# Maps of a differential attention summed without reciprocals, head outputs scaled on ScalarE, and a one-operation rope rotation

## The chip, the core and the metric

One core of a Trainium2 chip runs the whole kernel. The metric is the device time of one execution in microseconds (us), lower is better. Engines are named as the profile names them: PE is TensorE, DVE is VectorE, ACT is ScalarE, POOL is GpSimd, SP is SyncE, which issues most DMAs.

## The reference

The kernel computes one decoder layer on 512 tokens of 1024 features: a recurrent branch and a differential attention branch from one input projection, merged by gates, then a squared-ReLU MLP. The attention is what the change touches. Each of 8 heads has two softmax maps over the same values, and the second map is subtracted with a learned factor before the head's RMS norm:

```python
q = apply_rope(rms_norm(q.reshape(B, S, N_HEADS, 2, HEAD_DIM)) * q_norm_gain[l], cos, sin)
...
lam = (jnp.exp(jnp.sum(lambda_q1[l] * lambda_k1[l])) - jnp.exp(jnp.sum(lambda_q2[l] * lambda_k2[l])) + lam_init)
...
s = jnp.einsum("bhcqd,bhckd->bhcqk", qi, kt).astype(jnp.float32) * scale
p = jax.nn.softmax(jnp.where(mask, s, -jnp.inf), axis=-1)
attn = p[:, :, 0] - lam * p[:, :, 1]
o = jnp.einsum("bhqk,bhkv->bhqv", attn, vt)
...
o = rms_norm(o) * subln_gain * (1.0 - lam_init)

def apply_rope(x, cos, sin):
    x1, x2 = x[..., : HEAD_DIM // 2], x[..., HEAD_DIM // 2:]
    return jnp.concatenate([x1 * cos - x2 * sin, x2 * cos + x1 * sin], axis=-1)
```

## The kernel before

All large products run on PE as three fp32r matmuls each (`mm3`, L127 to L131): every operand is split into a high and a low part. For weights `load_w` (L114 to L125) does this: a DMA brings 128x1024 floats, ACT casts them to `wh` (L122) and DVE subtracts to get `wl` (L123), both at high priority. Nearly every 24 matmuls of 128x512 need one such pair, so ACT and DVE serve PE all through the program.

Until about 170 us the kernel projects the inputs of the recurrent branch and the first quarter of q and k. `qk_quarter` (L509 to L537) makes a quarter token-major in four tiles `raw` of 128x512, and turns each by the rope: L528 is issued twice for a tile, once for each half of 32 of every 64 columns (the halves swapped times the sine table, into `qsq`), L530 multiplies by the cosine, L531 adds, and a reciprocal square root of 32 columns (`rsqrt`, L84 to L100) scales the tile in L535. Quarter 0 is done before 124 us, quarters 1, 2 and 3 later. `qk_transpose` (L539 to L567) turns the tiles by PE (L547).

From about 170 to 447 us the 8 heads run (`heads`, L720 to L751), interleaved with other PE work that `fill` (L696 to L718) hands out by the table `PLAN`: gates `gm`, scans of the recurrent branch (L461, L462, L471), the other quarters, the values, the projection of the recurrent branch. `UNITS` sets how much of it is emitted between two steps of a head. Then the order on each engine is a list scheduler's, which takes instructions by priority and by estimated readiness, so that one edit can move many neighbours.

Each head has four steps `i`, for 128 queries each, with n = 128, 256, 384 or 512 keys. `softmax_step` (L572 to L598): PE makes the two maps of scores (`sc`), DVE adds the mask and finds the row's extreme (L587, into `e` and `nm`), ACT takes the exponential and its row sum (L589), DVE forms the reciprocals of both sums (L593) and the coefficient `cc` = s0 · nlam / s1 (L595), and L596 sums the maps as e0 + cc·e1. The result is s0 times the wanted map. `weights_t` transposes it by PE (L604, `aT`) and copies it out on ACT (odd steps, L607) or DVE (even steps, L609); `value_step` multiplies with the values (`po`, L615). A step's transposes and values come one step later in the program, so that PE has other work meanwhile.

`head_norm` (L618 to L636) ends a head: ACT copies the 128x512 output (`o`, L622) and takes four row sums of squares of 128x128 (`osq`, L625); DVE multiplies them by the squared reciprocals (L629, L630), takes the reciprocal square root (ten small operations, L89 to L99), multiplies by the reciprocal again (L633) and scales the output in one operation of 128x512 (L635). `head_out` (L638 to L647) transposes it by PE (L642, `yT`) in the next head's third step; for head 7 only after the gates that are left.

Of the kernel before, what the change touches and what calls it, by code (L numbers as in the profile page):

```python
# [20 lines left out]
AF = mybir.ActivationFunctionType  # L21
ALU = mybir.AluOpType
AX = mybir.AxisListType

P = 128
# [3 lines left out]
TB = S // P  # L29
# [24 lines left out]
def build(tc, out, x, xT_in, c, pos, vecs, reps, ada, w_xr, w_xr7, w_qk, w_v, w_gr, w_gm, w_lru,  # L54
# [4 lines left out]
    with ExitStack() as es:  # L59
# [18 lines left out]
        def tiny(name, n, dt=F32):  # L78
            return tmp.tile([P, n], dt, name=name, tag=f"s{n}", bufs=4 if n >= 32 else 12)
# [5 lines left out]
        def rsqrt(dst, src, n, mul, eps, name):  # L85

            eng = nc.vector
            v = tiny(name + "v", n)
            eng.tensor_scalar(v, src, mul, eps, op0=ALU.mult, op1=ALU.add)  # L89
            y = tiny(name + "y0", n, I32)  # L90
# [418 lines left out]
        def qk_quarter(qt):  # L509
# [10 lines left out]
            for t in range(TB):  # L520
                raw = rot[t]
                sqt = t_(f"qsq{qt}_{t}", tag="r")
                nc.scalar.activation(sqt, raw, AF.Square)
                nc.vector.tensor_reduce(s2[:, t * 8:t * 8 + 8], g8(sqt), axis=AX.X, op=ALU.add)
                r4, s4 = v4(raw), v4(sqt)
                for hf in range(2):
                    a, b = slice(hf * 32, hf * 32 + 32), slice(32 - hf * 32, 64 - hf * 32)
                    nc.vector.tensor_tensor(s4[:, :, :, a], r4[:, :, :, b],  # L528
                                            st[:, t, :, None, a].to_broadcast([P, 2, 4, 32]), op=ALU.mult)
                nc.vector.tensor_tensor(r4, r4, ct[:, t, :, None, :].to_broadcast([P, 2, 4, 64]), op=ALU.mult)  # L530
                nc.vector.tensor_tensor(raw, raw, sqt, op=ALU.add)  # L531
# [39 lines left out]

        def softmax_step(hd, q, k, i, rr):  # L572

            n = (i + 1) * P
            nn = max(n, 256)
            qc = slice(i * P, (i + 1) * P)
            sums = tiny(f"sm{hd}_{i}", 2)
            es_ = []
# [5 lines left out]
            for m in range(2):  # L584
# [4 lines left out]
                nc.scalar.activation(e[:, :n], e[:, :n], AF.Exp, bias=nm, scale=-1.0,  # L589
                                     accum_out=sums[:, m:m + 1])  # L590
                es_.append(e)
            rc = rr[:, 2 * i:2 * i + 2]
            nc.vector.reciprocal(rc, sums)  # L593
            cc = tiny(f"cc{hd}_{i}", 1)
            nc.vector.scalar_tensor_tensor(cc, sums[:, 0:1], nlam, rc[:, 1:2], op0=ALU.mult, op1=ALU.mult)  # L595
            nc.vector.scalar_tensor_tensor(es_[0][:, :n], es_[1][:, :n], cc, es_[0][:, :n],  # L596
# [20 lines left out]

        def head_norm(hd, po, rr):  # L618

# [4 lines left out]
            for t in range(TB):  # L624
                nc.scalar.activation(osq[:, t * P:(t + 1) * P], o1[:, t * P:(t + 1) * P], AF.Square,  # L625
                                     accum_out=os_[:, t:t + 1])
            r0 = rr[:, 0:8:2]
            o2 = tiny(f"o2{hd}", 4)
            nc.vector.tensor_tensor(o2, r0, r0, op=ALU.mult)  # L629
            nc.vector.tensor_tensor(o2, o2, os_, op=ALU.mult)  # L630
            orr = tiny(f"or{hd}", 4)
            rsqrt(orr, o2, 4, 1.0 / P, EPS, f"or{hd}")
            nc.vector.tensor_tensor(orr, orr, r0, op=ALU.mult)  # L633
            o3 = lambda t: t.rearrange("p (a b) -> p a b", b=P)
            nc.vector.tensor_tensor(o3(o1), o3(o1), orr[:, :, None].to_broadcast([P, TB, P]), op=ALU.mult)  # L635
            return o1  # L636
# [83 lines left out]
        def heads():  # L720
# [5 lines left out]
            for hd in range(NH):  # L726
                while hd // 2 not in qks or hd // 4 not in vs:
                    yield "need"
                q, k = qks[hd // 2][hd % 2]
                rr = tiny(f"rr{hd}", 8)  # L730
                po = None
                for i in range(TB):
                    a = softmax_step(hd, q, k, i, rr)
                    yield hd
# [13 lines left out]
                todo = []  # L748
                out_ = head_norm(hd, po, rr)
                yield hd  # L750
# [387 lines left out]
```

## Time and profile before

| | |
|---|---|
| median of 3 runs | 877.9 us (876.23 to 878.12) |
| the profiled execution | 876.41 us |
| its span | 874.6 us, so 1.81 us lie around it |
| granted TensorE clock | 1.00 in every slice |
| busy PE, DVE, ACT | 861.0, 651.5, 449.2 us |
| chain that ended last | PE 86%, DVE 10%, ACT 1%, DMA 1% |

PE is busy for 98% of the span; nearly 7 us of its idle time lie in the first 12 us and 3 us in the last 15. A matmul of 128x512 is shown as longer than the distance to the next, since the rows of two overlap; so an idle entry ahead of one shows only what of a wait is over that overlap. DVE and ACT are idle for a quarter and a half of the span on average, but not evenly: there are stretches in which both are full. The chain names DVE where the last thing before a matmul was a DVE result.

### The profile page before, as it was taken

How to read it: one execution, taken by the hardware profiler on the slowest of the kernel's cores; microseconds unless marked ns; L12 is line 12 of the kernel's file. 1: busy time of each engine (PE TensorE's matmuls, PEld its weight loads, DVE VectorE, ACT ScalarE, POOL GpSimd, SP SyncE). 2: the span in 40 equal slices, each digit the busy share in tenths (PEclk: the TensorE clock that was granted, in tenths of full speed). 3: DMA queues.
4: the chain of work that ended last, by engine and by line, in shares of the span. 5: the costliest groups of instructions: out<-in, count | busy, mean ns of one | idle time of the engine just before them, and what ended most of it. 6: DMA issues, size and time to landing. Idle time of an engine off the chain costs nothing.

```text
span 874.6 us, 11292 instructions
## 1 busy us (share of the span) xinstructions
PE 861.0 (98%) x4012; PEld 705.5 (81%) x4012; DVE 651.5 (74%) x1251; ACT 449.2 (51%) x748; POOL 15.1 (2%) x50
## 2 busy tenths in 40 slices
PE   6999999999999999999999999999999999999998
PEld 3888887877878888888888888888888888888887
DVE  6997995599859855786758556858766885876397
ACT  6673547985536543535623343747545544554461
POOL 1000000000000000000000000000000000002110
PEclk9999999999999999999999999999999999999999
DMA  8979425412255372238336332822641344139572
GB/s 315 370 250 319 152 97 134 136 68 73 87 131 169 99 191 76 93 87 227 110 126 210 132 121 75 273 87 72 193 148 70 128 161 169 49 126 235 120 122 96
DMA packets 64572, 128.92 MB, mean 147 GB/s; under 512 B 6146, under 2 KB 30850, under 8 KB 64516
## 3 DMA queue, kind: packets, MB, share of 16 engines
q1 hardware_dynamic: 59236, 122.97, 43.3%
q0 software_dynamic: 5280, 5.24, 3.9%
q8 instruction: 31, 0.51, 0.2%
q14 instruction: 25, 0.20, 0.1%
HBM read 113.51 MB, written 2.10 MB: 132 GB/s over the span
## 4 chain that ended last, share of the span: by engine, by line
PE 86%; DVE 10%; DMA 1%; issue 1%; ACT 1%; SPq 1%; ACTq 0%; DVEq 0%
PE f L131 6%; PE f L129 6%; PE f L130 6%; PE X L131 3%; PE X L130 3%; PE X L129 3%; PE gm L129 3%; PE gm L130 3%; PE gm L131 3%; DVE wl L123 2%; PE sc L582 2%; PE qk L131 2%; PE qk L129 2%; PE qk L130 2%; PE xr L129 2%; PE pr L129 2%
## 5 line engine op out<-in xcount | busy, mean ns | idle before, releaser
L122 ACT CAST wh<-w 128x1024 fp32r<-128x1024 f32 (+1 forms) x113 | 118.0, 1044 | 214.5 <-issue 48.1
L123 DVE TENSOR_TENSOR wl<-w,wh 128x1024 fp32r<-128x1024 f32 (+1 forms) x113 | 137.0, 1213 | 68.1 <-ACT wh L122 64.5
L131 PE MATMUL f<-h2h,wl 128*128 128x512 f32 x240 | 93.5, 390 | 0.4 <-DVE wl L123 0.4
L130 PE MATMUL f<-h2l,wh 128*128 128x512 f32 x240 | 93.2, 389 | 0.0
L129 PE MATMUL f<-h2h,wh 128*128 128x512 f32 x240 | 92.9, 390 | 0.0
L131 PEld LDWEIGHTS f<-h2h,wl 128*128 128x128 f32 x240 | 45.0, 188 | 10.1 <-DVE wl L123 0.8
L130 PEld LDWEIGHTS f<-h2l,wh 128*128 128x128 f32 x240 | 45.1, 188 | 9.4
L129 PEld LDWEIGHTS f<-h2h,wh 128*128 128x128 f32 x240 | 45.0, 188 | 9.3
L130 PE MATMUL gm<-hl,wh 128*128 128x512 f32 x128 | 51.0, 398 | 0.0
L129 PE MATMUL qk<-wh,hh 128*128 128x512 f32 x128 | 50.7, 396 | 0.0
L129 PE MATMUL gm<-hh,wh 128*128 128x512 f32 x128 | 50.5, 394 | 0.0
L131 PE MATMUL gm<-hh,wl 128*128 128x512 f32 x128 | 50.5, 394 | 0.0
L131 PE MATMUL qk<-wh,hl 128*128 128x512 f32 x128 | 50.4, 394 | 0.0
L130 PE MATMUL qk<-wl,hh 128*128 128x512 f32 x128 | 50.4, 394 | 0.0
L941 DVE TENSOR_TENSOR p_1l<-b,p_1h 128x1024 fp32r<-128x1024 f32 x24 | 29.4, 1223 | 26.3 <-ACT p_1h L940 26.1
L589 ACT ACTIVATE e<-e,nm 128x128 f32<-128x128 f32 (+3 forms) x64 | 35.7, 559 | 24.4 <-DVE nm L587 24.4
L940 ACT CAST p_1h<-b 128x1024 fp32r<-128x1024 f32 x24 | 25.2, 1051 | 31.0 <-PE f L130 22.9
L941 DVE TENSOR_TENSOR p_0l<-b,p_0h 128x1024 fp32r<-128x1024 f32 x24 | 29.3, 1223 | 15.0 <-ACT p_0h L940 13.8
L587 DVE CUSTOM_DVE_ANT_0 e<-sc,mask 128x128 f32<-128x128 f32 (+3 forms) x64 | 30.3, 484 | 9.9 <-PE sc L582 9.9
L940 ACT CAST p_0h<-b 128x1024 fp32r<-128x1024 f32 x24 | 25.3, 1055 | 24.2 <-PE X L131 12.4
L188 DVE CUSTOM_DVE_ANT_0 ada<-ada,cb,bada 128x1024 f32<-128x1024 f32 x16 | 20.5, 1283 | 14.3 <-DMA ada<-in_ada 14.1
L984 DVE TENSOR_TENSOR b<-b,b 128x1024 f32<-128x1024 f32 x24 | 29.1, 1220 | 0.1
(444 smaller groups left out, 2216.9 us busy)
## 6 DMA issues: line engine op xcount, KB each, us to landing
ada<-in_ada SPq DMA_DIRECT2D x64, 256.0 KB, 5.8
w<-in_w_ff SPq DMA_DIRECT2D x32, 512.0 KB, 3.2
b<-in_w_ff SPq DMA_DIRECT2D x30, 512.0 KB, 3.4
w<-in_w_qk SPq DMA_DIRECT2D x16, 512.0 KB, 3.2
w<-in_w_gm SPq DMA_DIRECT2D x16, 512.0 KB, 3.7
ada<-in_ada SPq DMA_DIRECT2D x16, 512.0 KB, 3.3
b_t<-in_w_ff POOLq DMA_DIRECT2D x10, 512.0 KB, 6.5
w<-in_w_gr SPq DMA_DIRECT2D x8, 512.0 KB, 4.0
```

Source lines behind the costliest of these rows:

```text
L122: i_w = nc.scalar.copy(wh[:, :n], w[:, :n])
L123: nc.vector.tensor_tensor(wl[:, :n], w[:, :n], f32(wh)[:, :n], op=ALU.subtract)
L129: nc.tensor.matmul(ps, lh, rh, start=first, stop=False, skip_group_check=more)
L130: nc.tensor.matmul(ps, lh, rl, start=False, stop=False, skip_group_check=more)
L131: nc.tensor.matmul(ps, ll, rh, start=False, stop=last, skip_group_check=more)
L188: nc.vector.tensor_tensor_reduce(w, w, cb, 1.0, bada[:, col:col + 1], op0=ALU.mult, op1=ALU.add, accum_out=mod[:, col:col + 1])
L582: nc.tensor.matmul(ps[m][:, :nn], q[m][:, qc], k[m][r][:, :nn], start=r == 0, stop=r == 1)
L587: nc.vector.tensor_tensor_reduce(e[:, :n], ps[m][:, :n], mask[:, S - n:], 1.0, 1e30, op0=ALU.add, op1=ALU.min, accum_out=nm)
L589: nc.scalar.activation(e[:, :n], e[:, :n], AF.Exp, bias=nm, scale=-1.0, accum_out=sums[:, m:m + 1])
L940: nc.scalar.copy(v4(wh), v)
L941: nc.vector.tensor_tensor(v4(wl), v, f32(v4(wh)), op=ALU.subtract)
L984: nc.vector.tensor_tensor(d, d, s_, op=ALU.add)
```

## The change

In `rsqrt` the first scaling is left out if no factor is given. In the rope one 128x512 operation, which reads the swapped halves through a reversed axis, takes the place of the two of 128x256. In `softmax_step` the maps are summed without reciprocals, as s1·e0 + (nlam·s0)·e1: ACT scales `e0` by s1 in place and forms `cc` = nlam·s0, so L593 and L595 are gone. The result is now s0·s1 times the wanted map, and `head_norm` sets it right: the small number of the norm is multiplied by (s0·s1)², in three operations on 128x4, and the output is scaled by ACT, four times 128x128. Lines of the change are shifted by up to two against those before.

```diff
--- before.py
+++ after.py
@@ -85,8 +85,10 @@
         def rsqrt(dst, src, n, mul, eps, name):
 
             eng = nc.vector
-            v = tiny(name + "v", n)
-            eng.tensor_scalar(v, src, mul, eps, op0=ALU.mult, op1=ALU.add)
+            v = src
+            if mul is not None:
+                v = tiny(name + "v", n)
+                eng.tensor_scalar(v, src, mul, eps, op0=ALU.mult, op1=ALU.add)
             y = tiny(name + "y0", n, I32)
             eng.tensor_scalar(y, v.bitcast(I32), -0.5, float(RSQRT_MAGIC), op0=ALU.mult, op1=ALU.add)
             y = y.bitcast(F32)
@@ -523,10 +525,9 @@
                 nc.scalar.activation(sqt, raw, AF.Square)
                 nc.vector.tensor_reduce(s2[:, t * 8:t * 8 + 8], g8(sqt), axis=AX.X, op=ALU.add)
                 r4, s4 = v4(raw), v4(sqt)
-                for hf in range(2):
-                    a, b = slice(hf * 32, hf * 32 + 32), slice(32 - hf * 32, 64 - hf * 32)
-                    nc.vector.tensor_tensor(s4[:, :, :, a], r4[:, :, :, b],
-                                            st[:, t, :, None, a].to_broadcast([P, 2, 4, 32]), op=ALU.mult)
+                sw = lambda t: t.rearrange("p m g (h d) -> p m g h d", h=2)
+                nc.vector.tensor_tensor(sw(s4), sw(r4)[:, :, :, ::-1, :],
+                                        sw(st[:, t, :, None, :].to_broadcast([P, 2, 4, 64])), op=ALU.mult)
                 nc.vector.tensor_tensor(r4, r4, ct[:, t, :, None, :].to_broadcast([P, 2, 4, 64]), op=ALU.mult)
                 nc.vector.tensor_tensor(raw, raw, sqt, op=ALU.add)
             rq = tiny(f"rq{qt}", 32)
@@ -569,12 +570,11 @@
         def att(name, dt=F32):
             return t_(name, dt, "a")
 
-        def softmax_step(hd, q, k, i, rr):
+        def softmax_step(hd, q, k, i, sums):
 
             n = (i + 1) * P
             nn = max(n, 256)
             qc = slice(i * P, (i + 1) * P)
-            sums = tiny(f"sm{hd}_{i}", 2)
             es_ = []
             ps = [bank(f"sc{hd}_{i}_{m}", "sc", 2) for m in range(2)]
             for m in range(2):
@@ -587,12 +587,11 @@
                 nc.vector.tensor_tensor_reduce(e[:, :n], ps[m][:, :n], mask[:, S - n:], 1.0, 1e30,
                                                op0=ALU.add, op1=ALU.min, accum_out=nm)
                 nc.scalar.activation(e[:, :n], e[:, :n], AF.Exp, bias=nm, scale=-1.0,
-                                     accum_out=sums[:, m:m + 1])
+                                     accum_out=sums[:, 2 * i + m:2 * i + m + 1])
                 es_.append(e)
-            rc = rr[:, 2 * i:2 * i + 2]
-            nc.vector.reciprocal(rc, sums)
+            nc.scalar.activation(es_[0][:, :n], es_[0][:, :n], AF.Copy, scale=sums[:, 2 * i + 1:2 * i + 2])
             cc = tiny(f"cc{hd}_{i}", 1)
-            nc.vector.scalar_tensor_tensor(cc, sums[:, 0:1], nlam, rc[:, 1:2], op0=ALU.mult, op1=ALU.mult)
+            nc.scalar.activation(cc, sums[:, 2 * i:2 * i + 1], AF.Copy, scale=nlam)
             nc.vector.scalar_tensor_tensor(es_[0][:, :n], es_[1][:, :n], cc, es_[0][:, :n],
                                            op0=ALU.mult, op1=ALU.add)
             return es_[0]
@@ -615,7 +614,7 @@
                 nc.tensor.matmul(po[:, i * P:n], aT[:, j * P:(j + 1) * P], v[j][:, vc * P:(vc + 1) * P],
                                  start=(j == 0), stop=(j == i))
 
-        def head_norm(hd, po, rr):
+        def head_norm(hd, po, sums):
 
             o1 = t_(f"o1{hd}")
             os_ = tiny(f"os{hd}", 4)
@@ -624,15 +623,16 @@
             for t in range(TB):
                 nc.scalar.activation(osq[:, t * P:(t + 1) * P], o1[:, t * P:(t + 1) * P], AF.Square,
                                      accum_out=os_[:, t:t + 1])
-            r0 = rr[:, 0:8:2]
-            o2 = tiny(f"o2{hd}", 4)
-            nc.vector.tensor_tensor(o2, r0, r0, op=ALU.mult)
-            nc.vector.tensor_tensor(o2, o2, os_, op=ALU.mult)
+            pp = tiny(f"op{hd}", 4)
+            nc.vector.tensor_tensor(pp, sums[:, 0:8:2], sums[:, 1:8:2], op=ALU.mult)
+            nc.vector.scalar_tensor_tensor(pp, pp, EPS, pp, op0=ALU.mult, op1=ALU.mult)
+            v = tiny(f"orv{hd}", 4)
+            nc.vector.scalar_tensor_tensor(v, os_, 1.0 / P, pp, op0=ALU.mult, op1=ALU.add)
             orr = tiny(f"or{hd}", 4)
-            rsqrt(orr, o2, 4, 1.0 / P, EPS, f"or{hd}")
-            nc.vector.tensor_tensor(orr, orr, r0, op=ALU.mult)
-            o3 = lambda t: t.rearrange("p (a b) -> p a b", b=P)
-            nc.vector.tensor_tensor(o3(o1), o3(o1), orr[:, :, None].to_broadcast([P, TB, P]), op=ALU.mult)
+            rsqrt(orr, v, 4, None, None, f"or{hd}")
+            for t in range(TB):
+                ob = o1[:, t * P:(t + 1) * P]
+                nc.scalar.activation(ob, ob, AF.Copy, scale=orr[:, t:t + 1])
             return o1
 
         def head_out(hd, o1):
@@ -727,10 +727,10 @@
                 while hd // 2 not in qks or hd // 4 not in vs:
                     yield "need"
                 q, k = qks[hd // 2][hd % 2]
-                rr = tiny(f"rr{hd}", 8)
+                sums = tiny(f"sm{hd}", 8)
                 po = None
                 for i in range(TB):
-                    a = softmax_step(hd, q, k, i, rr)
+                    a = softmax_step(hd, q, k, i, sums)
                     yield hd
                     if i == 0:
                         po = bank(f"po{hd}", "o", 1)
@@ -746,7 +746,7 @@
                     d()
                     yield hd
                 todo = []
-                out_ = head_norm(hd, po, rr)
+                out_ = head_norm(hd, po, sums)
                 yield hd
             y_att[NH - 1] = head_out(NH - 1, out_)
```

The order of the instructions moves too. First ACT at head 0, steps 0 and 1 (names: e, head, step, map; L589 the exponentials, L685 a gate, L460 and L462 a part of a scan, wh a weight's cast). Before:

```order
L589 ACTIVATE e0_0_0_1758,sm0_0_1750<-e0_0_0_1758,nm0_0_0_1757 128x128
L589 ACTIVATE e0_0_1_1762,sm0_0_1750<-e0_0_1_1762,nm0_0_1_1761 128x128
L685 ACTIVATE m0_0_1769<-gm0_1776 128x512
L460 ACTIVATE r0_1395<-r0_1395,sp8_705 128x512
L122 CAST wh28_1966<-w28_1964 128x1024
L589 ACTIVATE e0_1_0_1811,sm0_1_1803<-e0_1_0_1811,nm0_1_0_1810 128x256
L589 ACTIVATE e0_1_1_1815,sm0_1_1803<-e0_1_1_1815,nm0_1_1_1814 128x256
L460 ACTIVATE r1_1442<-r1_1442,sp8_705 128x512
L685 ACTIVATE m0_1_1869<-gm1_1876 128x512
```

With the change:

```order
L589 ACTIVATE e0_0_0_1753,sm0_1745<-e0_0_0_1753,nm0_0_0_1752 128x128
L589 ACTIVATE e0_0_1_1757,sm0_1745<-e0_0_1_1757,nm0_0_1_1756 128x128
L594 ACTIVATE cc0_0_1761<-sm0_1745,nlam_633 128x1
L592 ACTIVATE e0_0_0_1753<-e0_0_0_1753,sm0_1745 128x128
L685 ACTIVATE m0_0_1764<-gm0_1771 128x512
L124 CAST wh28_1958<-w28_1956 128x1024
L589 ACTIVATE e0_1_0_1805,sm0_1745<-e0_1_0_1805,nm0_1_0_1804 128x256
L589 ACTIVATE e0_1_1_1809,sm0_1745<-e0_1_1_1809,nm0_1_1_1808 128x256
L594 ACTIVATE cc0_1_1813<-sm0_1745,nlam_633 128x1
L592 ACTIVATE e0_1_0_1805<-e0_1_0_1805,sm0_1745 128x256
L462 ACTIVATE r0_1391<-r0_1391,sp8_705 128x512
```

Each step's coefficient and scaling come on ACT behind its second exponential, ahead of the gate and the cast.

Second, DVE at head 0, step 2: from the second map's mask to the sum of the maps (L596 before, L595 now; xc are the scans). Before:

```order
L587 ISA e0_2_1_1855,nm0_2_1_1854<-sc0_2_1_1845,mask_104 128x384
L587 ISA nm0_2_1_1854 128x1
L471 TENSOR_TENSOR xc1_1088<-xc1_1088,gel1_1086 128x512
L461 SCALAR_TENSOR_TENSOR xc2_1126<-r2_1563,xc2_1126 128x512
L123 TENSOR_TENSOR wl29_2109<-w29_2106,wh29_2108 128x1024
L143 TENSOR_TENSOR yl1_1841<-xc1_1088,yh1_1839 128x512
L593 RECIPROCAL rr0_1749<-sm0_2_1843 128x2
L462 SCALAR_TENSOR_TENSOR xc2_1126<-r2_1563,xc2_1126 128x512
L595 SCALAR_TENSOR_TENSOR cc0_2_1859<-sm0_2_1843,nlam_633,rr0_1749 128x1
L587 ISA e0_3_0_1943,nm0_3_0_1942<-sc0_3_0_1936,mask_104 128x512
L587 ISA nm0_3_0_1942 128x1
L596 SCALAR_TENSOR_TENSOR e0_2_0_1851<-e0_2_1_1855,cc0_2_1859,e0_2_0_1851 128x384
```

With the change:

```order
L587 ISA e0_2_1_1848,nm0_2_1_1847<-sc0_2_1_1838,mask_104 128x384
L587 ISA nm0_2_1_1847 128x1
L463 SCALAR_TENSOR_TENSOR xc0_1046<-r0_1391,xc0_1046 128x512
L463 SCALAR_TENSOR_TENSOR xc1_1084<-r1_1438,xc1_1084 128x512
L464 SCALAR_TENSOR_TENSOR xc0_1046<-r0_1391,xc0_1046 128x512
L464 SCALAR_TENSOR_TENSOR xc1_1084<-r1_1438,xc1_1084 128x512
L473 TENSOR_TENSOR xc0_1046<-xc0_1046,gel0_1044 128x512
L473 TENSOR_TENSOR xc1_1084<-xc1_1084,gel1_1082 128x512
L595 SCALAR_TENSOR_TENSOR e0_2_0_1844<-e0_2_1_1848,cc0_2_1852,e0_2_0_1844 128x384
```

Six operations of two scans now stand together between the mask and the sum, where before there were a part of two scans, a weight's subtraction, and the other map's masks.

Third, DVE at the end of quarter 1's rope: from the last sum of a rope (raw, L531 before) to the first scaled tile (L535 before), which PE transposes at 246.6 us. Before:

```order
L531 TENSOR_TENSOR raw1_3_2343<-raw1_3_2343,qsq1_3_2366 128x512
L95 TENSOR_TENSOR rq1a0_2378<-rq1y0_2376 128x32
L98 SCALAR_TENSOR_TENSOR rq1b0_2380<-rq1a0_2378,rq1v_2374 128x32
L123 TENSOR_TENSOR wl37_2727<-w37_2724,wh37_2726 128x1024
L99 SCALAR_TENSOR_TENSOR rq1y1_2381<-rq1b0_2380,rq1y0_2376 128x32
L95 TENSOR_TENSOR rq1a1_2384<-rq1y1_2381 128x32
L98 SCALAR_TENSOR_TENSOR rq1b1_2386<-rq1a1_2384,rq1v_2374 128x32
L99 SCALAR_TENSOR_TENSOR rq1y2_2387<-rq1b1_2386,rq1y1_2381 128x32
L95 TENSOR_TENSOR rq1a2_2390<-rq1y2_2387 128x32
L98 SCALAR_TENSOR_TENSOR rq1b2_2392<-rq1a2_2390,rq1v_2374 128x32
L99 SCALAR_TENSOR_TENSOR rq1_2373<-rq1b2_2392,rq1y2_2387 128x32
L535 TENSOR_TENSOR raw1_0_2337<-raw1_0_2337,rq1_2373 128x512
```

With the change:

```order
L532 TENSOR_TENSOR raw1_3_2335<-raw1_3_2335,qsq1_3_2355 128x512
L97 TENSOR_TENSOR rq1a0_2366<-rq1y0_2364 128x32
L100 SCALAR_TENSOR_TENSOR rq1b0_2368<-rq1a0_2366,rq1v_2362 128x32
L101 SCALAR_TENSOR_TENSOR rq1y1_2369<-rq1b0_2368,rq1y0_2364 128x32
L97 TENSOR_TENSOR rq1a1_2372<-rq1y1_2369 128x32
L100 SCALAR_TENSOR_TENSOR rq1b1_2374<-rq1a1_2372,rq1v_2362 128x32
L101 SCALAR_TENSOR_TENSOR rq1y2_2375<-rq1b1_2374,rq1y1_2369 128x32
L97 TENSOR_TENSOR rq1a2_2378<-rq1y2_2375 128x32
L100 SCALAR_TENSOR_TENSOR rq1b2_2380<-rq1a2_2378,rq1v_2362 128x32
L125 TENSOR_TENSOR wl37_2711<-w37_2708,wh37_2710 128x1024
L101 SCALAR_TENSOR_TENSOR rq1_2361<-rq1b2_2380,rq1y2_2375 128x32
L536 TENSOR_TENSOR raw1_0_2329<-raw1_0_2329,rq1_2361 128x512
```

The subtraction `wl37` comes at the end of the chain of small operations instead of near its start.

Fourth, ACT at the end of head 7, from the copy of its output. Before:

```order
L622 COPY o17_4694<-po7_4364 128x512
L625 ACTIVATE osq7_4697,os7_4695<-o17_4694 128x128 x4
L122 CAST wh65_4740<-w65_4738 128x1024
L685 ACTIVATE thg14_4628<-gm14_4635 128x512
L122 CAST wh66_4781<-w66_4779 128x1024
L685 ACTIVATE thg15_4661<-gm15_4668 128x512
L644 ACTIVATE yah7_4734<-yT7_4729,sg_636 128x512
```

With the change:

```order
L621 COPY o17_4660<-po7_4333 128x512
L124 CAST wh65_4708<-w65_4706 128x1024
L685 ACTIVATE thg14_4594<-gm14_4601 128x512
L624 ACTIVATE osq7_4663,os7_4661<-o17_4660 128x128 x4
L635 ACTIVATE o17_4660<-o17_4660,or7_4673 128x128 x3
L124 CAST wh66_4749<-w66_4747 128x1024
L685 ACTIVATE thg15_4627<-gm15_4634 128x512
L635 ACTIVATE o17_4660<-o17_4660,or7_4673 128x128
L644 ACTIVATE yah7_4702<-yT7_4697,sg_636 128x512
```

The squares come behind a cast and a gate instead of ahead of them, and the four scalings are new. On PE the transposes `yT` of head 7 stand behind 44 gate matmuls after the last value matmul before, and behind 26 now:

```order
L129 MATMUL gm15_4668<-hh7_554,wh64_4664 128x512
L130 MATMUL gm15_4668<-hl7_558,wh64_4664 128x512
L131 MATMUL gm15_4668<-hh7_554,wl64_4665 128x512
L642 MATMUL yT7_4729<-ident_99,o17_4694 128x128 x4
L129 MATMUL pa0_4744<-yah0_2161,wh65_4740 128x512
```

With the change:

```order
L131 MATMUL gm15_4634<-hh7_554,wh64_4630 128x512
L132 MATMUL gm15_4634<-hl7_558,wh64_4630 128x512
L133 MATMUL gm15_4634<-hh7_554,wl64_4631 128x512
L642 MATMUL yT7_4697<-ident_99,o17_4660 128x128 x3
L131 MATMUL pa0_4712<-yah0_2152,wh65_4708 128x512
L132 MATMUL pa0_4712<-yal0_2154,wh65_4708 128x512
L133 MATMUL pa0_4712<-yah0_2152,wl65_4709 128x512
L131 MATMUL pa0_4712<-yah1_2649,wh65_4708 128x512
L132 MATMUL pa0_4712<-yal1_2651,wh65_4708 128x512
L133 MATMUL pa0_4712<-yah1_2649,wl65_4709 128x512
L131 MATMUL pa0_4712<-yah2_3052,wh65_4708 128x512
L132 MATMUL pa0_4712<-yal2_3054,wh65_4708 128x512
L642 MATMUL yT7_4697<-ident_99,o17_4660 128x128
L133 MATMUL pa0_4712<-yah2_3052,wl65_4709 128x512
```

Three of the transposes come at the same place as the four before, the fourth after eight more matmuls.

## Rows read from the trace of the kernel before

**Rows 1.** The page: busy time by engine.

```profile
PE 861.0 (98%) x4012; PEld 705.5 (81%) x4012; DVE 651.5 (74%) x1251; ACT 449.2 (51%) x748; POOL 15.1 (2%) x50
```

**Rows 2.** Timeline of PE: start, duration, instruction, [idle before, releaser]; 124 to 247 us.

```profile
124.51 0.50 PE L131 MATMUL gr<-hh,wl 128*128 128x512 f32 x1 [0.18 <-DVE wl L123]
124.84 0.39 PE L129 MATMUL gr<-hh,wh 128*128 128x512 f32 x1
125.07 0.39 PE L130 MATMUL gr<-hl,wh 128*128 128x512 f32 x1
...
182.42 0.44 PE L604 MATMUL aT<-ident,e 128*128 128x128 f32 x2 [0.19 <-DVE e L596]
...
191.18 0.52 PE L604 MATMUL aT<-ident,e 128*128 128x128 f32 x3 [0.66 <-DVE e L596]
...
195.61 0.63 PE L604 MATMUL aT<-ident,e 128*128 128x128 f32 x4 [0.44 <-DVE e L596]
...
210.08 0.66 PE L642 MATMUL yT<-ident,o 128*128 128x128 f32 x4 [0.38 <-DVE o L635]
...
217.97 0.63 PE L604 MATMUL aT<-ident,e 128*128 128x128 f32 x4 [0.19 <-DVE e L596]
...
246.60 0.30 PE L547 MATMUL qT<-ident,raw 128*128 128x128 f32 x1 [0.74 <-DVE raw L535]
```

**Rows 3.** Windows 170 to 200: PE, PEld, DVE, ACT, POOL busy us (count); clock, DMA.

```profile
170.00:180.00 10.00, 10.00 (x48) 8.09 (x47) 9.01 (x20) 9.86 (x21) 0.00 (x0) 1.00 0.16 54
180.00:190.00 10.00, 9.81 (x46) 7.77 (x45) 10.00 (x21) 8.52 (x17) 0.00 (x0) 1.00 0.25 82
190.00:200.00 10.00, 8.90 (x53) 7.10 (x52) 9.91 (x25) 6.77 (x19) 0.00 (x0) 1.00 0.21 76
```

**Rows 4.** Timeline of DVE: the rope of one tile.

```profile
103.50 0.76 DVE L528 TENSOR_TENSOR qsq<-raw,st 128x256 f32<-128x256 f32 x2
...
105.31 0.69 DVE L530 TENSOR_TENSOR raw<-raw,ct 128x512 f32<-128x512 f32 x1
```

**Rows 5.** Timeline of ACT and DVE: a weight split ahead of 247 us.

```profile
241.36 1.06 ACT L122 CAST wh<-w 128x1024 fp32r<-128x1024 f32 x1 [1.53 <-PE qk L131]
...
243.05 1.22 DVE L123 TENSOR_TENSOR wl<-w,wh 128x1024 fp32r<-128x1024 f32 x1
```

**Rows 6.** Timeline of DVE: reciprocal and coefficient among other work, head 0.

```profile
179.97 0.16 DVE L593 RECIPROCAL rr<-sm 128x2 f32<-128x2 f32 x1
180.04 1.20 DVE L462 TENSOR_TENSOR_SCAN xc<-r,xc 128x512 f32<-128x512 f32 x1
181.16 0.19 DVE L595 SCALAR_TENSOR_TENSOR cc<-sm,nlam,rr 128x1 f32<-128x1 f32 x1
181.28 0.69 DVE L471 TENSOR_TENSOR xc<-xc,gel 128x512 f32<-128x512 f32 x1
```

**Rows 7.** Lines of ACT by form: count, busy us, mean ns, idle before.

```profile
L256 ACT ACTIVATE x<-x,rs 128x512 f32<-128x512 f32 x3 | 1.9, 713 | 0.0
L256 ACT ACTIVATE x<-x,rs 128x128 f32<-128x128 f32 x5 | 1.7, 395 | 1.9 <-DVE rs L236 1.9
L174 ACT ACTIVATE warm<-eps_t 128x1 f32<-128x1 f32 x1 | 0.2, 203 | 0.0
```

**Rows 8.** Timeline of DVE: end of head 7.

```profile
439.06 0.16 DVE L630 TENSOR_TENSOR o<-o,os 128x4 f32<-128x4 f32 x1 [2.82 <-ACT osq L625]
439.25 0.17 DVE L89 TENSOR_SCALAR or7v<-o 128x4 f32<-128x4 f32 x1
...
442.72 0.69 DVE L635 TENSOR_TENSOR o<-o,or 128x512 f32<-128x512 f32 x1
```

**Rows 9.** Timeline of PE: the transposes of head 7.

```profile
446.95 0.60 PE L642 MATMUL yT<-ident,o 128*128 128x128 f32 x4
```

**Rows 10.** Timeline of ACT: end of head 7.

```profile
437.12 0.59 ACT L622 COPY o<-po 128x512 f32<-128x512 f32 x1 [1.25 <-PE po L615]
437.74 0.31 ACT L625 ACTIVATE osq<-o 128x128 f32<-128x128 f32 x1
```


## The prediction

> **What bounds the kernel now.** I read the page's busy times first: PE is busy 861.0 of 874.6 us, DVE 651.5, ACT 449.2 [rows 1]. So the change, which takes work from DVE, adds some to ACT and leaves PE's matmuls as they are, can only gain where PE waits for DVE, and lose where it will wait for ACT. Next I read PE's timeline for those waits. From 120 to 250 us, where the touched code first runs, seven show, all ended by DVE: one for a weight's subtraction at 124.51, four for a sum of two maps (`aT`), one for a scaled head (`yT`), one for a scaled rope tile at 246.60 [rows 2]. From 250 us to the last stretch PE shows no such wait. A matmul of 128x512 lasts 0.39 us but the next starts 0.23 later (124.84 to 125.07), so each wait is 0.16 longer than its bracket. The brackets sum to 2.78 us; with 7 x 0.16 it is **3.9 us, all that the change could win**. The third view, the windows, shows why the waits are there: DVE is full (9.91 to 10.00 of 10 us) from 180 to 200 us, and ACT, half idle over the program, has only 0.14, 1.48 and 3.23 us free in the three windows from 170 us, 4.85 in all [rows 3]. Both are crowded at heads 0 and 1.
>
> The sum below is made against the profiled execution, 876.41 us, which is 1.5 below the median of the three runs, 877.9. A difference counts from 0.2%, 1.8 us.
>
> **The rope.** Per tile the two half operations take 0.76 us together, one plain 128x512 multiplication 0.69 [rows 4]. No row has a reversed operand. Its lower bound is the plain one, a gain of 0.07; its upper bound, if reversal halves the rate, about 1.2, since 0.6 of the 0.69 is streaming, a loss of 0.5. I take the plain price: the halves already read and write broken rows of 32 columns, and two of them cost what one piece of twice the size does. Four tiles stand ahead of the wait at 124.51: the chain there is four times 0.07 shorter, **-0.28** of a wait of 0.34. The Trainium skill, in VectorE: DVE Perf Modes, section Mode 1× (REGULAR), says that this mode makes one result per cycle for fp32 and odd strides alike; the row of the halves agrees (0.76 for 512 columns), a reversed axis no run here shows. By it the price is the plain one, and the loss below falls away.
>
> **The wait at 246.60.** It is 0.74 + 0.16 = 0.90 long, so PE arrived at about 245.7 [rows 2]. Ahead of it on DVE the change saves four times 0.07 of rope and head 1's scaling of the output (0.69, or 0.6 among others). The weight's subtraction, which stood early in the chain at 243.05 and lasts 1.22 [rows 5], now comes near its end. Its cast starts at 241.36 and lasts 1.06, so the subtraction can start at 242.5; then 1.15, one small operation (0.2), and the first tile (0.69) end at 244.6 at the earliest. By the DVE chain alone (246.45 less 0.9) they end at 245.6. Either is ahead of PE: **-0.85**.
>
> **The four steps of heads 0 and 1.** Removed from DVE: the reciprocal, after which the next operation starts 0.07 later, and the coefficient, 0.12 [rows 6]: 0.19 per step where DVE has other work, 8 x 0.19 = 1.5 us in the crowded stretch, and 0.6 for head 0's output. Added to ACT: the coefficient, 0.20 by the only 128x1 row, and a scaling, 0.40 for 128 columns to 0.71 for 512 [rows 7], each some 0.1 less in a queue: 0.2 + 0.30, 0.2 + 0.40, 0.2 + 0.51 and 0.2 + 0.61, 2.6 us a head. So the sum of the maps gets rid of 0.2 (0.4 where DVE stands idle) ahead of it and gets 0.5 to 0.8 instead. I laid the durations of the rows on the new order. Longest are two waits: at head 0, step 2, six scan operations now stand between the mask and the sum, two of each kind (starting 0.6, 1.12 and 0.6 apart), 4.6 us, so the sum ends some 0.8 after PE is there, as before (0.82 at 191.18); and at head 1, step 0, the coefficient and scaling stand behind head 0's copy and squares, some 0.65. Others are 0.1 to 0.5. My nine waits sum to 3.6 us. The five of before are 1.86 + 5 x 0.16 = 2.66, and waits under 0.16, which don't show, may add half a microsecond. I take **+0.4**; the bounds are -2.7 (all vanish) and +2.8 (second rival).
>
> **The end of head 7.** Before, the output is ready at 442.72 + 0.69 = 443.4 [rows 8], 3.5 us ahead of its transposes at 446.95 [rows 9], which 44 gate matmuls of 0.23 put off from 436.83. Now 26 stand there: PE comes 26 x 0.23 = 6.0 after 436.83, that is 5.7 after ACT's copy began (437.12 [rows 10]). From that start: copy 0.5, a cast 0.95 and a gate 0.5 that now come ahead, squares to the first DVE operation 1.3 (437.74 to 439.06), eleven small dependent operations at 0.19 to 0.2 (439.06 to 439.25), 2.2: 5.45. The scalings then come 0.3 apart, the first done at 5.9, the third at 6.5, where the third transpose would be due at 5.9. A cover of 3.5 us becomes a wait of **+0.6**. The fourth transpose is hidden by eight matmuls, 1.8 us. Were the cast not ahead, it would be nothing; were another one ahead of the scalings, 1.6.
>
> **Costed at nothing:** heads 2 to 7, both edits. PE waits nowhere there, with a step's transposes put off behind other work; ACT's 3.8 us more a head (2.6 and four output scalings of 0.31) fall into a queue that is about half idle. If this cover were gone, each step would cost 0.3 to 0.4. The shorter norm (`rsqrt` without its first operation, one more ahead) is off the path except at the end. DMAs are as many as before.
>
> **Sum:** -0.28 - 0.85 + 0.4 + 0.6 = -0.13: 876.3 for the profiled execution, 877.8 for the median, **no measurable change**.
>
> **Rivals.** *All waits on DVE vanish.* The crowded stretch loses 2.1 us of DVE work, most of the waits there (2.7), and the end stays covered. For it: each of the seven was ended by DVE [rows 2]. Against: the path through ACT is longer, and the end's order has moved. With all gone it is 877.9 - 3.9 = 874.0; with half of those at heads 0 and 1 left, 875.3.
>
> *ACT's queue becomes the bound (slower).* The sum of the maps must wait for a scaling that stands behind casts, gates and scan steps on an engine with 4.85 us free in 30 [rows 3]. The path is 0.50, 0.60, 0.71 and 0.81 instead of 0.2 to 0.4: 0.35 a step, 8 x 0.35 = 2.8, and the end costs 1.6 with one more cast ahead; with the gains at 124 and 246, 2.8 + 1.6 - 1.1 = +3.3, **881.2**. It decides as soon as the scaling ends after PE has reached the step's transposes, which in my walk it does at three of eight steps. The Trainium skill speaks for it: ScalarE: Activation LUTs, section Rules for kernel authors, says of multiplications "Use VectorE, not ScalarE", with a ratio for bf16 only. The rows agree in fp32: 0.69 for 512 columns on DVE, four times 0.40 on ACT [rows 7, 8]. Against it stands ACT's idle half over the program.
>
> *The one-operation rope is no saving.* If the reversed axis runs at half rate, +0.5 for each of four tiles ahead of 124 and of 246: 4.0 instead of -1.1, and with the other terms (+1.0) +5.0, 882.9. For it: no row shows such an operand. Against: the broken rows cost nothing.
>
> **Numbers.** Forecast 0.45 (876.1 to 879.7 with no change seen), all waits vanish 0.27, ACT bounds 0.22, rope 0.06. The likeliest time is 877.8. The range leaves out the rope case and the far ends of the other two: 874.4 to 881.2. Faster by over 0.2% is the first rival, 0.27; within, 0.45; slower, the other two, 0.28.
>
> **What would show it.** In the profile after: no wait at 124 above 0.1, the rope's operation at 0.69 and none at 246; waits of 2.5 to 4 us in all between 176 and 220 us, some of them now ended by DVE's sum late behind ACT's scaling; a wait of about 0.6 at head 7's transposes; none from 250 to 435 us. The prediction is wrong if the waits at heads 0 and 1 sum to under 2 or over 5 us, if heads 2 to 7 show waits, or if the rope's operation takes over 0.8.

## The result and the profile after

The change makes the kernel **slower by 0.6%**: 882.91 us (882.37 to 884.06, 6 runs) against 877.29 (876.23 to 878.12, 6 runs), ratio 1.0062 with a 95% interval of 1.0052 to 1.0072. The forecast was no measurable change, 877.8, with a range up to 881.2. The profiled execution took 882.96 us, 6.55 more than that of before.

The page of the changed kernel, busy times by engine, against [rows 1]:

```profile
PE 867.5 (98%) x4012; PEld 707.0 (80%) x4012; DVE 637.9 (72%) x1155; ACT 478.7 (54%) x844; POOL 15.1 (2%) x50
```

DVE lost 13.6 us and ACT gained 29.5 (the prediction's 3.8 a head make some 30 for eight heads). But PE, whose matmuls are the same 4012, is busy 6.5 us longer, and that is the whole loss: its idle time is what it was. So the waits come next. PE's timeline of the changed kernel, the waits that show between 180 and 260 us and the end of head 7, against [rows 2, 9]:

```profile
186.35 0.41 PE L603 MATMUL aT<-ident,e 128*128 128x128 f32 x2 [0.81 <-DVE e L595]
...
201.57 0.33 PE L603 MATMUL aT<-ident,e 128*128 128x128 f32 x1 [0.32 <-DVE e L595]
...
208.10 0.33 PE L642 MATMUL yT<-ident,o 128*128 128x128 f32 x1 [0.23 <-ACT o L635]
...
213.94 0.44 PE L603 MATMUL aT<-ident,e 128*128 128x128 f32 x2 [0.56 <-DVE yal L646]
...
245.70 0.30 PE L548 MATMUL qT<-ident,raw 128*128 128x128 f32 x1 [0.71 <-DVE raw L536]
...
448.26 0.91 PE L642 MATMUL yT<-ident,o 128*128 128x128 f32 x3
```

The waits of heads 0 and 1 are other ones, with much the same sum; the one at 246 us is still there (at 245.70), and the transposes of head 7 start within the overlap but take 0.91 for three instead of 0.60 for four. None of this is 6 us. Time against work tells where those went. I added up, matmul by matmul, the usual distance from start to start, and compared the time at which both kernels reach the same sum:

| PE's time before, us | 132 | 237 | 300 | 442 | 462 | 502 | 542 | 603 | 703 | 803 | 863 |
|---|---|---|---|---|---|---|---|---|---|---|---|
| lag of the change, us | 0.0 | 0.3 | 0.3 | 1.1 | 2.0 | 3.0 | 3.8 | 4.1 | 4.9 | 6.0 | 6.5 |

Up to the end of the heads the change is 1.1 us behind, 2.0 past head 7's transposes. Then it loses 0.4 to 0.5 us in every 20 up to 540 us and 0.1 to 0.2 after that, in code that the change doesn't touch and where PE hardly ever waits. The windows view (window, PE busy and count, granted clock, DMA share, GB/s) of 455 to 535 us, where PE runs the products `pa` and `wo`, before:

```profile
455.00:535.00 80.00, 80.00 (x354) 1.00 0.42 142
```

and with the change:

```profile
455.00:535.00 80.00, 80.00 (x346) 1.00 0.42 135
```

PE is full in both, the granted clock is 1.00 in both (its higher level), and eight matmuls fewer fit in. The timeline shows it one by one; before, the first and the last of 18 in a row:

```profile
469.73 0.39 PE L131 MATMUL pa<-yah,wl 128*128 128x512 f32 x1
...
473.58 0.39 PE L130 MATMUL pa<-yal,wh 128*128 128x512 f32 x1
```

and with the change, of 15:

```profile
470.02 0.40 PE L131 MATMUL pa<-yah,wh 128*128 128x512 f32 x1
...
473.27 0.40 PE L133 MATMUL pa<-yah,wl 128*128 128x512 f32 x1
```

17 steps in 3.85 us are 226 ns each, 14 in 3.25 are 232. By product, the mean distance from start to start in ns:

| product | moving operand | weights | before | after | lost, us |
|---|---|---|---|---|---|
| f (240 x 3) | h2 | wh, wl | 226.8 | 227.3 | 0.4 |
| gr | h | wh, wl | 226.8 | 226.9 | 0.0 |
| pr | y | wh, wl | 228.8 | 232.3 | 0.6 |
| pa | ya | wh, wl | 227.3 | 232.3 | 1.0 |
| wo | m | wh, wl | 226.7 | 232.3 | 1.1 |
| X, Y, Z on p_0 | p_0 | a, s | 226.7 | 227.6 | 0.3 |
| X, Y, Z on p_1 | p_1 | a, s | 226.7 | 232.7 | 1.9 |

With 0.3 from two smaller products, those at 232 ns and more lose 4.9 us. The 0.7 us of `f` and of X, Y, Z on p_0 are a slow start, not a rate: nine times `f` follows X, Y, Z on p_1, and its first eight steps there are 224 to 236 ns in the mean of the nine, 231 over all; behind p_1 the first three steps on p_0 are 231 to 233. After that both are at 227. In the kernel before these steps are at 227 from the first. What the products at 232 share is not a tile but a pair. The compiled programs say where the tiles lie (bytes in a partition):

```
                     before   after
wh (first buffer)     40672   40672
p_1h                  40672   40672
h2h                   59104   59104
small tiles of 2 columns (sm, 12 x 32 bytes)   116064 to 116447   none
small tiles of 8 columns (rr before, sm after)  115680  115680
yh (first buffer)    116448  116064
s2l (first buffer)   194272  193888
p_0h                 206560  206176
```

The change replaces the `sums` tiles of two columns by one of eight, so the tag for two columns, 12 buffers of 8 bytes that take 32 each, is no longer allocated. All that is allocated behind moves down by 384 bytes: the moving operands of `pr`, `pa` and `wo` (they share the buffers of yh), the weights `a` and `s` and the buffer p_0. `wh`, `wl`, `h` and p_1 (which lies in the buffers of `wh`) stay. Of the products in the table, exactly those whose two operands lie on different sides of the gap are slow.

### The profile page after: what moved, and what is told of

The parts are those of the page before. It is cut to its first block, busy times and chain, and to the rows that moved or that the text cites. A ratio compares the mean times of both kernels' runs of the same rounds, so it can differ in the third digit from the quotient of the medians.

```text
span 881.2 us, 11273 instructions
## 1 busy us (share of the span) xinstructions
PE 867.5 (98%) x4012; PEld 707.0 (80%) x4012; DVE 637.9 (72%) x1155; ACT 478.7 (54%) x844; POOL 15.1 (2%) x50
## 4 chain that ended last, share of the span: by engine, by line
PE 85%; DVE 10%; DMA 1%; issue 1%; ACT 1%; SPq 0%; DVEq 0%; ACTq 0%
PE f L133 6%; PE f L131 6%; PE f L132 6%; PE X L133 3%; PE X L131 3%; PE X L132 3%; PE gm L131 2%; PE qk L133 2%; PE gm L132 2%; PE qk L132 2%; PE qk L131 2%; PE gm L133 2%; DVE wl L125 2%; PE sc L582 2%; PE pr L131 2%; PE wo L133 2%
## 5 line engine op out<-in xcount | busy, mean ns | idle before, releaser
L589 ACT ACTIVATE e<-e,nm 128x128 f32<-128x128 f32 (+3 forms) x64 | 35.6, 558 | 21.1 <-DVE nm L587 20.8
L131 PEld LDWEIGHTS gm<-hh,wh 128*128 128x128 f32 x128 | 24.2, 189 | 4.9 <-ACT thg L685 0.5
```

What stands on the lines that cost most here:

```text
L131: nc.tensor.matmul(ps, lh, rh, start=first, stop=False, skip_group_check=more)
```

## The experiments

The first three kernels test this against the theory that the change's own work costs the time; the others ask what about the placement counts and what the change's own work is worth.

**The change with the 384 bytes put back.** The edit is one unused tile; the order on every engine stays that of the change.

```diff
-            todo, out_ = [], None
+            todo, out_, pad = [], None, tmp.tile([P, 96], F32, name="pad", tag="pad", bufs=1)
```

> The change with an unused tile of 384 bytes per partition beside the small tiles, so that everything allocated behind them lies where it lay before; the order on every engine is that of the change. Placement theory (the change dropped the 12 small buffers of 32 bytes each of the tag for two columns, 384 bytes, and so moved the operands of pr, pa, wo and half of X, Y, Z against the weights; such matmuls start 232 ns apart instead of 227): about 878.3 us, 1.0 over the kernel before, with pa and wo at 227 ns again. Work theory (the longer path over ScalarE and the new order cost the 5.6 us): 882.9, pa and wo still at 232.

Measured: 877.76 us (11 runs), ratio to before 1.0010 (1.0002 to 1.0019). Its window at 455 us:

```profile
455.00:535.00 80.00, 80.00 (x355) 1.00 0.42 140
```

355 matmuls again, and `pa`, `wo` at 227 ns. So the placement costs about 5 of the 5.6 us, and what is left for the change's own work is 0.9 (0.2 to 1.7; the runs of before beside it are other ones than those of the result).

**The kernel before with 128 bytes more**, in the same place (`[P, 32]`):

> The kernel before with nothing but an unused tile of 128 bytes per partition beside the small tiles; same order. Placement theory, if the distance of the two operands counts by its remainder by 512 (minus 384 and plus 128 have the same): pa, wo, pr and the X, Y, Z on p_1 at 232 ns, 882.3 us, 5.1 slower than before. Work theory: 877.3, no difference, 227 ns.

Measured: 882.47 us (5 runs), ratio 1.0063 (1.0049 to 1.0077): the whole loss, without any line of the change.

```profile
455.00:535.00 80.00, 80.00 (x346) 1.00 0.42 141
```

**With 256 bytes more** (`[P, 64]`):

> The kernel before with an unused tile of 256 bytes in the same place. Placement theory leaves two ways: if the remainder by 256 counts, 877.3 us and 227 ns; if that by 512 or more counts, slow matmuls, up to 5 us. Work theory: 877.3, 227 ns.

Measured: 876.60 us (11 runs), ratio 1.0000 (0.9991 to 1.0009).

```profile
455.00:535.00 80.00, 80.00 (x354) 1.00 0.43 146
```

So of the two remainders that by 256 decides, not that by 512, and it is not enough that something moved.

**A map of distances.** A kernel of nothing but groups of 48 matmuls, `nc.tensor.matmul(ps, W[:, wo + k * P:wo + k * P + P], M[:, mo:mo + S])` with eight slices of weights in turn.

> No part of the layer: only groups of 48 matmuls of 128x512 in the form of this kernel, with eight weight slices of 512 bytes taken in turn, and within a group one distance between the moving and the stationary operand, in bytes by the remainder: da 0, db 32, dc 64, dd 96, de 128, df 160, dg 192, dh 224, di 256, dj 384, dk 512, dl 640, dm 1024, dn 1664; then sa with the weights shifted by 128 instead, sb with both shifted by 128, sc with the weights by 256, sd with the weights by 64, se with both by 64. Placement theory, with the remainder by 256: 227 ns from start to start for da, di, dk, dm, sb, sc, se and 232 for de, dj, dl, dn, sa; the others open. Rival, that an operand's own address counts and not the distance: sb as slow as de. Rival, that the slow matmuls in the kernel come from something else than the addresses: all groups alike.

PE's timeline of it (start, duration of the group):

```profile
19.07 11.04 PE L83 MATMUL da<-M,W 128*128 128x512 f32 x48
29.95 11.37 PE L83 MATMUL db<-M,W 128*128 128x512 f32 x48
41.16 11.16 PE L83 MATMUL dc<-M,W 128*128 128x512 f32 x48
52.16 11.37 PE L83 MATMUL dd<-M,W 128*128 128x512 f32 x48
63.37 11.36 PE L83 MATMUL de<-M,W 128*128 128x512 f32 x48
74.57 11.40 PE L83 MATMUL df<-M,W 128*128 128x512 f32 x48
85.81 11.35 PE L83 MATMUL dg<-M,W 128*128 128x512 f32 x48
97.00 11.35 PE L83 MATMUL dh<-M,W 128*128 128x512 f32 x48
108.19 11.05 PE L83 MATMUL di<-M,W 128*128 128x512 f32 x48
119.08 11.36 PE L83 MATMUL dj<-M,W 128*128 128x512 f32 x48
...
174.44 11.36 PE L83 MATMUL sa<-M,W 128*128 128x512 f32 x48
185.64 11.06 PE L83 MATMUL sb<-M,W 128*128 128x512 f32 x48
196.54 11.04 PE L83 MATMUL sc<-M,W 128*128 128x512 f32 x48
207.42 11.36 PE L83 MATMUL sd<-M,W 128*128 128x512 f32 x48
218.62 11.08 PE L83 MATMUL se<-M,W 128*128 128x512 f32 x48
```

From one group's start to the next's are 48 steps: 10.88 us, 226.7 ns, at distance 0 (da); 11.2, 233 ns, at 32, 128 and 192 (db, de, dg) and as well at 96, 160, 224, 384, 640 and 1664; 10.9 at 256 (di), at 512 and at 1024; 11.0, 229 ns, at 64 (dc). With both operands shifted by 128 it is fast (sb, 10.90), with the weights alone shifted, slow (sa, 11.20): the distance counts and not an address. With the weights shifted by 64, which makes the distance minus 64 or 192, it is slow (sd): the sign counts. With both shifted by 64 the group is nearly fast (se, 227.5): its first ten steps are 224 to 236, the rest 227. The other groups at 227 that follow one at 233 have such a slow start as well (one step in di and sc, three in dk, dm and sb).

**64 bytes in the kernel** (`[P, 16]` in the kernel before), a single run:

> The kernel before with 64 bytes more per partition beside the small tiles, to see whether the map of distances carries over with its sign: pr, pa and wo, whose moving operand lies behind the small tiles, have a distance of 64 and should start 229 ns apart (dc in the map), X, Y, Z on p_1, whose weights lie behind them, have 192 and should start 233 apart (dg, sd). If the sign does not count: both alike.

Measured: 880.32 us, 3.1 more than the median of before, and in the window a count between 354 and 346:

```profile
455.00:535.00 80.00, 80.00 (x350) 1.00 0.41 142
```

X, Y, Z on p_1 start 233.3 apart in the mean, `wo` 225.9, 229.1 and 231.7 for its three kinds, 228.9 in the mean: as the map said, with its sign. The three values are not those of three kinds of operands: in the map's group dc, which has one kind, the steps go 226, 229, 232 in turn too. What the expectation left out are X, Y, Z on p_0, whose two operands both lie 64 bytes further, at the distance of before: 229.0 instead of 226.7. They come in groups of twelve, of which the first five steps are slow behind p_1, and the first ten behind `f`, as in se. Since `f` itself is fast, a slow start doesn't need a slow product ahead of it.

**Whose reads collide?** A second kernel of matmuls alone.

> No part of the layer: groups of 48 matmuls in a row with 512 moving columns, to see what collides. ga: distance 0 bytes, gb 128, both with 128 columns of weights; gc and gd the same with 64 columns of weights, ge and gf with 32. Theory that the load of the next weights beside the stream is what is slowed or slows: gb some 6.5 ns over ga, gd about half of that over gc, gf about a quarter over ge. Rival, that the stream by itself is slow at such addresses: the same 6 to 7 ns in all three pairs. gg alternates two weight tiles W and V, both at distance 0; gh has V at 128 (W at 0); gi has the moving operand and V shifted by 128, so that W is at 128 and V at 0. If the loading beside the stream counts, in gh the matmul that uses W (while the next weights, of V, are loaded) is the slow one, 233 against 227, and in gi the one that uses V; if the weights in use count, the other way round.

The first six groups on PE's timeline:

```profile
21.83 11.04 PE L83 MATMUL ga<-M,W 128*128 128x512 f32 x48
32.71 11.36 PE L83 MATMUL gb<-M,W 128*128 128x512 f32 x48
43.91 11.19 PE L83 MATMUL gc<-M,W 128*64 128x512 f32 x48
54.94 11.17 PE L83 MATMUL gd<-M,W 128*64 128x512 f32 x48
65.95 11.27 PE L83 MATMUL ge<-M,W 128*32 128x512 f32 x48
77.05 11.25 PE L83 MATMUL gf<-M,W 128*32 128x512 f32 x48
```

Measured, from start to start: 227.1 (ga, the mean of its two groups) and 233.3 (gb) with 128 columns of weights; 229.9 and 229.4 with 64 (gc, gd); 231.3 and 231.1 with 32 (ge, gf). With narrower weights the distance makes no difference, but the matmuls are at 229 to 231 either way. Where good and bad weights alternate, both kinds are slow: 232.2 with W and 234.5 with V in gh, 231.7 and 233.3 in gi; where two good ones alternate (gg) it is 226 to 228 after the first nine steps. Neither theory gave this, so **why the distance counts stays open**. That it counts only beside a full load of 128 columns of weights speaks for the load. The alternation did not single it out; with the slow starts seen above it may not be able to, since in gh and gi no matmul is more than one step from a bad one. That is argued and not shown.

**The rope alone**, in the kernel before, with the change's three lines for L526 to L529:

> The kernel before with only the rope's rotation in one operation; nothing is allocated otherwise. Placement theory: matmuls at 227 ns, and no more than the rope's own gain, 876.3 to 877.3 us, the operation at 0.69 us. Rival, the reversed read at half rate: 1.2 us for the operation and 881 us.

Measured: 876.60 us (11 runs), ratio 0.9999 (0.9990 to 1.0007); the operation takes 677 to 693 ns.

What is left is the change's own 0.9 us. **Outputs scaled by DVE again**, with the 384 bytes put back:

```diff
-            for t in range(TB):
-                ob = o1[:, t * P:(t + 1) * P]
-                nc.scalar.activation(ob, ob, AF.Copy, scale=orr[:, t:t + 1])
+            o3 = lambda t: t.rearrange("p (a b) -> p a b", b=P)
+            nc.vector.tensor_tensor(o3(o1), o3(o1), orr[:, :, None].to_broadcast([P, TB, P]), op=ALU.mult)
```

> The change with the 384 bytes put back, and the heads' outputs scaled by VectorE in one operation as before (maps still summed without reciprocals, rope in one operation). If what is left of the change's cost, about 0.9 us, is the end of head 7, where the scaling on ScalarE comes behind a cast: the transposes of head 7 wait no more, since the squares come straight behind the copy in this order, 877.2 us. If it is the sum of the maps on ScalarE: no better than 877.8.

Measured: 875.93 us (11 runs), ratio 0.9988 (0.9979 to 0.9997), faster than before and by more than expected. The ACT timeline at the end of head 7, first of the change, then of this kernel:

```profile
442.34 0.59 ACT L621 COPY o<-po 128x512 f32<-128x512 f32 x1 [1.25 <-PE po L614]
442.82 1.05 ACT L124 CAST wh<-w 128x1024 fp32r<-128x1024 f32 x1
443.77 0.60 ACT L685 ACTIVATE thg<-gm 128x512 f32<-128x512 f32 x1
444.26 0.31 ACT L624 ACTIVATE osq<-o 128x128 f32<-128x128 f32 x1
...
447.80 0.99 ACT L635 ACTIVATE o<-o,or 128x128 f32<-128x128 f32 x3 [2.27 <-DVE or L101]
```

```profile
441.12 0.58 ACT L621 COPY o<-po 128x512 f32<-128x512 f32 x1
441.73 0.31 ACT L624 ACTIVATE osq<-o 128x128 f32<-128x128 f32 x1
```

With the change the squares come 1.9 us behind the copy's start, and the scalings end at 448.8, while the transposes were due at 448.1; here the squares come 0.6 behind it. But the transposes still wait a little, against the expectation: PE starts them 0.47 behind the last gate matmul instead of 0.23.

```profile
445.86 0.39 PE L133 MATMUL gm<-hh,wl 128*128 128x512 f32 x1
446.33 0.63 PE L641 MATMUL yT<-ident,o 128*128 128x128 f32 x4
```

So the end of head 7 explains a part of the difference to the change with its tiles put back (877.76). It doesn't explain why this kernel is faster than the one before, where the transposes wait for nothing.

**Only the order at the end of head 7**, the cast behind the squares, outputs still on ACT:

```diff
+            if last_sq[0] is not None:
+                after(i_w, last_sq[0])
...
+            if hd == NH - 1:
+                last_sq[0] = i_q
```

> The change with the 384 bytes put back, outputs still scaled by ScalarE, and only the order at the end of head 7 altered: the weight's cast comes behind the squares instead of ahead. By the sum (copy 0.5, gate 0.5, squares 1.3, eleven small operations 2.2, two scalings 0.7 = 5.2, PE there at 5.7) the wait of 0.7 at head 7's transposes goes: 877.1 us. If the wait comes from something else, the transposes still wait 0.5 to 0.7 and it is 877.8.

Measured: 877.35 us (11 runs), ratio 1.0003 (0.9994 to 1.0012). The expected 0.7 did not come: the transposes still wait, 0.27 ahead of the first and 0.2 ahead of the second, 0.5 in all, where the change waits 0.6, since the cast that was put behind the squares brought its subtraction into the middle of DVE's chain of small operations:

```profile
444.90 0.16 DVE L97 TENSOR_TENSOR or7a<-or7y 128x4 f32<-128x4 f32 x1
445.01 1.22 DVE L125 TENSOR_TENSOR wl<-w,wh 128x1024 fp32r<-128x1024 f32 x1
446.15 0.15 DVE L100 SCALAR_TENSOR_TENSOR or7b<-or7a,orv 128x4 f32<-128x4 f32 x1
...
446.93 0.16 DVE L101 SCALAR_TENSOR_TENSOR or<-or7b,or7y 128x4 f32<-128x4 f32 x1
```

The chain ends at 447.1, 5.4 after the copy's start (441.64) and not 4.5. The intervals of this kernel (0.9994 to 1.0012) and of the change with its tiles put back (1.0002 to 1.0019) overlap, so the two can't be told apart.

**The maps alone**, rope and scaling as before, 384 bytes put back:

> The change with the 384 bytes put back and two of its parts undone: the rope in two operations and the heads' outputs scaled by VectorE, so that only the sum of the maps without reciprocals (with its norm) is left. If the maps' part is what makes the version with outputs on VectorE 1.2 us faster than before: 876.0 to 876.4. If the rope's part makes it: 877.1, as before.

Measured: 876.96 us (11 runs), ratio 1.0001 (0.9992 to 1.0010): no difference. By the expectation that would point at the rope, but the rope alone gained nothing either (0.9999). So neither the rope nor the maps alone can be told from the kernel before, and what makes the version with outputs on DVE faster stays open.

**Outputs on DVE with 128 bytes put back** (`[P, 32]`), so that all lies 256 lower than before:

> Outputs on VectorE, rope in one operation, maps without reciprocals, with 128 bytes put back instead of 384, so that the operands behind the small tiles lie 256 bytes lower than before. By the remainder by 256: as with 384, 875.9 us, matmuls at 227 ns. If a distance other than before's is slow by itself: 232 ns and 881.

Measured: 876.67 us (11 runs), ratio 0.9992 (0.9983 to 1.0001), with `pa` and `wo` at 227 ns. The remainder holds with a minus too. Beside the 0.9988 of the same program with 384 bytes, what the version with outputs on DVE gains over the kernel before is about 0.1%, no more than can just be told. With 384 bytes it is the fastest of those tried.

## Why the prediction was wrong

**The step that failed** stands in the first part: that the change "leaves PE's matmuls as they are" and so can only win or lose where PE waits. It costed instructions and their order and put nothing for where tiles lie. The runs show in its place that some 1,000 of the 4012 matmuls start 232 to 233 ns apart instead of 227 to 230, with PE busy 867.5 us instead of 861.0 and as idle as before; about 5 of the 5.6 us go when the tiles are put back. The diff showed the cause, a tile of two columns gone, but the profile of before doesn't show the risk: each product of the table has 227 to 229 ns there. The map of addresses of both programs, which needs no chip, shows the 384 bytes; what they cost could not be read anywhere.

**The terms**, measured in the change with the 384 bytes put back, whose matmuls run as before (by the lag of PE against the work; lines and times given are those of the change itself, which has the same waits):

- *The rope, -0.28 expected, 0 measured.* The operation has the plain price (0.69), so this reversed axis is free, and the rival that it runs at half rate falls, although its 882.9 us happens to be the measured time. But the wait at 124 us did not follow: with two operations it is there in four of five profiles (0.33 to 0.66 us), with one in three of six (0.25 to 0.35, 0.27 in the change). DVE waits for the `ada` transfers ahead of 90 us for 3.0 to 4.5 us, which differs from profile to profile by more than the 0.28 saved; that this decides about the wait is likely but not shown.
- *The wait at 246 us, -0.85 expected, 0 measured.* The DVE chain got shorter as the step had it, and the upper of my two estimates was right:

```profile
243.51 1.22 DVE L125 TENSOR_TENSOR wl<-w,wh 128x1024 fp32r<-128x1024 f32 x1
244.65 0.18 DVE L101 SCALAR_TENSOR_TENSOR rq<-rq1b,rq1y 128x32 f32<-128x32 f32 x1
244.87 1.29 DVE L536 TENSOR_TENSOR raw<-raw,rq 128x512 f32<-128x512 f32 x2
```

The first tile is ready at 245.6 instead of 246.4. But the transposes come earlier in PE's new order by as much, so the wait is 0.71 over the overlap, against 0.74. I compared DVE's new time with PE's old one.
- *Heads 0 and 1, +0.4 expected, +0.2 measured.* Six waits of 0.26 to 0.99, 3.2 in all (the walk gave 3.6); the longest is, as forecast, at head 0's step 2, behind the scans (0.81 over the overlap at 186.35). The rival that ACT's queue becomes the bound falls: the scalings are as priced (0.39 to 0.72) and `cc` is longer (0.29 for 0.20), but at five of the eight steps the scaling is done 0.65 to 2.5 us before DVE gets to the sum.
- *The end of head 7, +0.6 expected, +0.6 to 0.7 measured*, with the parts as worked out: copy, cast, gate, squares to the first DVE operation 3.23 us (442.34 to 445.57; 3.25 expected).
- *Heads 2 to 7, nothing expected, +0.4 measured*, in several small waits. By the prediction's own sign ("if heads 2 to 7 show waits") this was a miss.
- *What the change could win, 3.9.* One wait of before was overlooked: from 250 us on PE waits once more for a weight's subtraction, in `f`.

```profile
562.96 0.50 PE L131 MATMUL f<-h2h,wl 128*128 128x512 f32 x1 [0.36 <-DVE wl L123]
```

With 0.16 for the overlap it would make the bound 4.4. The sum isn't touched by it, since the change does nothing there.

So the walk was right to 0.4 us in most places and 0.85 off in one: -0.1 in the sum, where the change with its tiles put back shows +0.9 (0.2 to 1.7; the terms above add up to 1.2 in its profiled execution). That alone would have been the forecast case, no measurable change. What decided was outside it.

## What to carry to other kernels

Where the same cost per instruction changes in code that an edit doesn't touch, compare the time of one matmul by product, before looking for waits; a busy share of PE near 100% hides it (98% here in both). An edit that drops or adds a small tile moves every tile allocated behind it: for matmuls of this form keep the distance of the two operands a multiple of 256 bytes (here a pad of 384 or 128 bytes) and compare the addresses of both programs. And a walk over a new order needs both engines' new places: a chain that ends earlier gains nothing if the one that waits for it comes earlier too.

## What was unexpected in the hardware

- fp32r matmuls of 128x512 with a full load of weights start 227 ns apart when the moving and the stationary operand lie a multiple of 256 bytes apart in SBUF, and 233 to 234 ns apart at the other remainders tried (32, 96, 128, 160, 192, 224); 64 is in between, with 229. In this kernel some 1,000 such matmuls cost 5 us. Why is open.
- After a change to other operands up to ten of the first matmuls can be slow though their own distance is a good one (`f` behind X, Y, Z on p_1 in the changed kernel: 231 ns over eight steps, then 227).
- With weights of 64 or 32 columns the same matmuls start 229 to 231 ns apart at either distance, so fewer columns are not faster.
- A DVE multiplication that reads two halves of 32 columns in reversed order (each half forwards) takes what a plain one takes: 677 to 693 ns for 128x512.
